# First 256 tokens of the first two projection chunks taken unnormed, their norm factor multiplied into the results

## The chip, the cores and the metric

One core of a Trainium2 chip runs the program. The metric is the device time of one execution in microseconds, as the median of several runs. Lower is better. TensorE (PE) multiplies matrices, VectorE (DVE), ScalarE (ACT) and GpSimd (POOL) work element by element, SyncE (SP) issues most of the DMAs. Each engine works through its own queue in the order in which the instructions stand there; semaphores hold an instruction back until what it needs is done.

## The reference

A residual block of a streaming encoder over 512 tokens of 1024 features, in float32. Cut to what matters here:

```python
xn = rmsnorm(h, norm_mix_g)                   # per token: x * rsqrt(mean(x*x) + eps) * g
u  = xn @ w_in                                # 1024 x 7168
q, k, v, xr, gr, ga, gb = split(u)            # seven parts of 1024 columns
ya = chunked_band_attention(q, k, v) @ w_attn_out
xc = causal_depthwise_conv(xr, conv_w, conv_b)        # four taps over the tokens
yb = (rg_lru(xc, ...) * gelu(gr)) @ w_rnn_out
h  = h + (sigmoid(ga + ..) * ya + sigmoid(gb + ..) * yb) @ w_o
h  = h + swiglu(rmsnorm(h));  out = rmsnorm(h)
```

`rmsnorm` multiplies each token's row by one number, its norm factor, and each feature by g. The factor of a token commutes with the product with `w_in`; the factor g of a feature doesn't.

## The kernel before

**Tiles.** Tokens lie in four tiles of 128 rows, `xt[0]` to `xt[3]` (names `x` in the profile), features in eight slices of 128 (k = 0 to 7). The projection needs x with the features on the partitions: `xnT[k]` holds slice k of all 512 tokens. Every operand is kept as two parts, a high part rounded to a shorter format (`fp32r`) and a low part, the rest; a product is three matrix products, high by high, high by low, low by high (`mm3`, L78 to L84). High parts are made by ACT, low parts by DVE, as a subtraction.

**Chunks.** `w_in` is taken in chunks of 256 columns, in the order xr0, gr0, ga0, gb0, xr2 and so on. A chunk's weights come by two DMAs of 512 KB (`raw`, three buffers), are split into `whl` (four buffers), and make two result tiles of 128 columns in PSUM, c = 0 and 1. Result tiles named `po_...` take turns in the four banks of the tag "mm".

**The start (L472 to L798).** Tokens are handled in two halves of 256. The first half: ACT sums the squares of tile 0 (`first_sum`, L620), DVE and ACT those of half of tile 1 each (`second_sum`, L628; `root_of_second`, L634); roots and reciprocals give the factors `rs`; DVE and ACT scale the rows into `xs` (`scaled_rows`, L651; `second_rows`, L645). TensorE turns 128x128 blocks of `xs` by a product with the identity into banks of the tags "t" and "s" (`turned`, `transposed`, L662 to L674; `pt_mix` in the profile), and `parted` (L676) multiplies by g and splits into the high and low part of `xnT`. Until this is under way, sixteen products of zeros (`busy`, L479) keep TensorE at work. Then come the products of the first half of xr0, two slices at a time (`first_pair`, L726), and of gr0 (`first_half`, L705). The second half of the tokens follows the same way, with the second half of xr0 and gr0 after it.

**After the start.** L951 to L966: xr0 goes through the convolution (`conv_in` on ACT, three `conv_taps` on DVE, `conv_out` on ACT and POOL, which gives `xch`), gr0 through the gelu (`gelu_in`, `gelu_out`, L846 to L855), meanwhile the weights of ga0 and gb0 are split (`prefetch`, L423). TensorE goes on with ga0 (`po_ga`), the gate products of the recurrence (`rg`, L867, from `xch` and the weights `wrg`) and gb0 (`po_gb`).

**What sets the order.** In the stretches under `tc.manual_schedule` the named engines keep the order of the code there, and single instructions are tied by `tc.keep_in_program_order`; the rest is placed by a scheduler. A DMA on SP waits in SP's queue for its buffer, and holds all that stand behind it.

## Time and profile before

| | us |
|---|---|
| median of 3 runs (lowest, highest) | 842.54 (841.65, 842.77) |
| the profiled execution | 842.18 |
| its span | 840.4 |
| PE busy | 833.1 |
| DVE busy | 663.2 |
| ACT busy | 516.6 |
| POOL busy | 162.5 |

The span reaches from the first to the last instruction; the time of the execution has 1.78 us more around it. A row of the timeline gives the start in us from the start of the span, the duration, the engine, the line, the operation, the tiles that it writes and reads, and their shapes; equal instructions that follow each other are one row with their count. PEld is the loading of the stationary operand, which overlaps the products. SPq is SP's DMA queue: the row is the issue, not the transfer. A matrix product's duration includes its latency, so the distance between two starts says what each costs.

### The profile page before, as it was taken

The page shows a single profiled execution, that of the slowest core. Times are in us where ns is not written, and L with a number is a line of the kernel's source. Part 1 is how long each engine was busy: PE and PEld are TensorE (multiplying, and loading weights), DVE is VectorE, ACT ScalarE, POOL GpSimd, SP SyncE. Part 2 cuts the span into 40 slices and gives each one's busy share as a digit, 9 for nine tenths or more (in the row PEclk, how much of TensorE's full clock was granted, in tenths as well). Part 3 has the DMA queues.
Part 4 walks back from the last instruction along what each step waited for, and adds up shares of the span by engine and source line. Part 5 has one row for each costly group of instructions (what it writes and reads, how often), then busy time and mean ns, then how long its engine had stood idle before and what let it go on. Part 6 is the DMA issues. An engine that isn't in the chain of part 4 may idle for free.

```text
span 840.4 us, 11922 instructions
## 1 busy us (share of the span) xinstructions
PE 833.1 (99%) x4230; PEld 706.7 (84%) x4230; DVE 663.2 (79%) x976; ACT 516.6 (61%) x850; POOL 162.5 (19%) x219
## 2 busy tenths in 40 slices
PE   9999999999999999999999999999999999999997
PEld 7988888888888888888888888888888999988886
DVE  6678769887959788887568867888778878998784
ACT  7686848774356688878534557663764465455543
POOL 2502030231010043443212012005102321300000
PEclk9999999999999999999999999999999999999999
DMA  9566488653645444548458975555955576644442
GB/s 286 172 236 224 140 301 267 184 201 100 206 145 150 138 151 139 173 129 223 97 136 220 331 283 162 165 176 165 238 175 151 147 188 183 215 155 145 160 172 100
DMA packets 107323, 153.98 MB, mean 183 GB/s; under 512 B 8216, under 2 KB 66160, under 8 KB 106752
## 3 DMA queue, kind: packets, MB, share of 16 engines
q1 hardware_dynamic: 102304, 141.32, 51.7%
q0 software_dynamic: 3728, 8.96, 6.4%
q10 hardware_dynamic: 1232, 2.95, 0.9%
q8 instruction: 33, 0.54, 0.3%
q14 instruction: 26, 0.21, 0.1%
HBM read 139.53 MB, written 30.45 MB: 202 GB/s over the span
## 4 chain that ended last, share of the span: by engine, by line
PE 98%; DMA 0%; ACT 0%; DVE 0%; issue 0%; ACTq 0%
PE fu_x L84 2%; PE fu_x L83 2%; PE fu_x L80 2%; PE o L1201 2%; PE fg_x L84 2%; PE fg_x L83 2%; PE fg_x L80 2%; PE pT L1181 2%; PE s L1152 2%; PE po_gb L80 2%; PE po_ga L80 2%; PE po_gr L84 2%; PE po_gr L80 2%; PE po_gr L83 2%; PE po_k L80 2%; PE po_q L80 2%
## 5 line engine op out<-in xcount | busy, mean ns | idle before, releaser
L1165 ACT ACTIVATE p<-p,m 128x384 f32<-128x384 f32 (+2 forms) x64 | 35.8, 560 | 14.8 <-DVE m L1164 14.3
L1170 POOL TENSOR_SCALAR p<-p,rl 128x128 f32<-128x128 f32 (+3 forms) x61 | 38.0, 640 | 15.3 <-DVE rl L1166 13.8
L1422 POOL TENSOR_TENSOR sg<-sg,keep_fu_x 128x512 f32<-128x512 f32 x8 | 14.5, 1822 | 100.3 <-DVE keep_fu_x L1421 100.3
L89 DVE TENSOR_TENSOR pp<-pT,pp 128x384 fp32r<-128x384 f32 (+1 forms) x48 | 27.0, 598 | 4.5 <-ACT pp L88 3.3
L89 DVE TENSOR_TENSOR whl_fu_w<-raw_fu_w,whl_fu_w 128x1024 fp32r<-128x1024 f32 (+1 forms) x18 | 23.4, 1307 | 8.7 <-ACT whl_fu_w L88 8.7
L89 DVE TENSOR_TENSOR whl_fu_t<-t_fu,whl_fu_t 128x1024 fp32r<-128x1024 f32 (+1 forms) x18 | 24.8, 1390 | 5.1 <-ACT whl_fu_t L88 5.0
L812 POOL MEMSET bias<- 64x64 f32 x16 | 2.4, 147 | 135.9 <-DMA bias<-ext_d 135.8
L83 PE MATMUL po_gr<-xnT,whl_gr 128*128 128x512 f32 (+1 forms) x80 | 27.6, 347 | 0.0
L80 PE MATMUL po_gr<-xnT,whl_gr 128*128 128x512 f32 (+1 forms) x80 | 27.4, 348 | 0.0
L84 PE MATMUL po_gr<-xnT,whl_gr 128*128 128x512 f32 (+1 forms) x80 | 27.2, 346 | 0.0
L1164 DVE CUSTOM_DVE_ANT_0 p<-s,bias 128x384 f32<-128x384 f32 (+2 forms) x48 | 25.4, 552 | 1.5
L88 ACT ACTIVATE whl_fu_w<-raw_fu_w 128x1024 fp32r<-128x1024 f32 (+1 forms) x18 | 17.7, 987 | 13.5 <-issue 7.6
L80 PE MATMUL po_k<-xnT,whl_qk 128*128 128x512 f32 x64 | 25.5, 398 | 0.0
L80 PE MATMUL po_q<-xnT,whl_qk 128*128 128x512 f32 x64 | 25.5, 398 | 0.0
L80 PE MATMUL po_ga<-xnT,whl_ga 128*128 128x512 f32 x64 | 25.4, 397 | 0.0
L80 PE MATMUL po_gb<-xnT,whl_gb 128*128 128x512 f32 x64 | 25.2, 394 | 0.0
L84 PE MATMUL po_q<-xnT,whl_qk 128*128 128x512 f32 x64 | 25.0, 390 | 0.0
L83 PE MATMUL po_ga<-xnT,whl_ga 128*128 128x512 f32 x64 | 25.0, 390 | 0.0
L84 PE MATMUL po_k<-xnT,whl_qk 128*128 128x512 f32 x64 | 25.0, 390 | 0.0
L80 PE MATMUL po_yb<-rnn,whl_yb 128*128 128x512 f32 x64 | 24.9, 390 | 0.0
L83 PE MATMUL po_gb<-xnT,whl_gb 128*128 128x512 f32 x64 | 24.9, 390 | 0.0
L84 PE MATMUL po_ga<-xnT,whl_ga 128*128 128x512 f32 x64 | 24.9, 389 | 0.0
(693 smaller groups left out, 3072.2 us busy)
## 6 DMA issues: line engine op xcount, KB each, us to landing
raw_qk<-in_w_in_dram SPq DMA_DIRECT2D x32, 256.0 KB, 3.3
out_t<-in_w_ffn_out_dram SPq DMA_DIRECT2D x16, 512.0 KB, 5.2
raw_fu_w<-in_w_ffn_in_dram SPq DMA_DIRECT2D x16, 512.0 KB, 4.5
raw_fo<-in_w_ffn_out_dram SPq DMA_DIRECT2D x14, 512.0 KB, 4.2
...
```

Of the source, the lines that this page charges most:

```text
L80: ins = pe.matmul(o, sh, mh, start=start, stop=False, skip_group_check=parts)
L83: pe.matmul(o, sh, ml, start=False, stop=False, skip_group_check=parts)
L84: pe.matmul(o, sl, mh, start=False, stop=stop, skip_group_check=parts)
L88: act.activation(hi, src, AF.Copy)
L89: dve.tensor_sub(lo, src, f(hi))
L1152: pe.matmul(sc, qs, kk[:, part, e, 0:w], start=part == 0, stop=part == 1, skip_group_check=qb < 2)
L1164: dve.tensor_tensor_reduce(prob[qb][:], src, prob[0][:] if qb == 0 else bias[:, S - w:S], -1.0, 3e38, ALU.add, ALU.min, nmax[:, qb:qb + 1])
L1165: act.activation(prob[qb][:], prob[qb][:], AF.Exp, bias=nmax[:, qb:qb + 1], scale=-1.0, accum_out=lsum[:, qb:qb + 1])
L1170: eng.tensor_scalar(prob[qb][:], prob[qb][:], rl[:, qb:qb + 1], 1.0, ALU.mult, ALU.mult)
L1181: pe.transpose(pt[:, at * P:(at + 1) * P], prob[qb][:, kb * P:(kb + 1) * P], ident[:])
L1201: pe.matmul(po[:, S - n:S], st, pp[i][:, part, lo:lo + n], start=kb == 0 and part == 0, stop=kb == NT - 1 and part == 1)
L1422: (pool if keep and (unit != f_units[-1] or side) else dve).tensor_mul(o, o, keep_ if keep else bank)
```

## The change

The first half of the tokens is no longer scaled before it is turned. TensorE turns the rows of x themselves, first all blocks of tile 0, then of tile 1 (`turned_by_rows`); `parted` multiplies by g as before, so that `xnT` holds x times g for the first 256 tokens, without their norm factors. With that the first halves of xr0 and gr0 are computed. The factors, still from the sums of squares, are written to DRAM as a row of 256 numbers and read back onto all partitions (`by_token`, tile `rs_b`), and DVE multiplies them into the first 256 columns of the four result tiles in PSUM before the convolution and the gelu (`scaled_first_half`). For the later chunks the first half of `xnT` is put together again (`whole_of`: high plus low), multiplied by the factors (`scaled_whole`) and split anew in place (`split_whole`), four slices at a time.

Besides: eight `busy` products in place of sixteen; the first 512 KB of weights in two DMAs; the high part of its first two slices by DVE, not ACT; in the first `first_pair` the two products of high by high first; the loads of gr0 ahead of the last two tiles of x, and those of `wrg` (`gates_loaded`) behind the factors; the split of `wrg` later; the sums of the second tile of the half later; a few instructions after the start tied to the order of the code.

```diff
...
-    def load(name, k):
+    def load(name, k, pieces=1, tied=False):
...
         for src, col, width in parts:
-            sp.dma_start(out=raw[:, :, to:to + width],
-                         in_=src[at:at + n * P, col:col + width].rearrange("(k p) e -> p k e", p=P))
+            for a in range(0, n, n // pieces):
+                b = a + n // pieces
+                ins = sp.dma_start(out=raw[:, a:b, to:to + width],
+                                   in_=src[at + a * P:at + b * P, col:col + width].rearrange("(k p) e -> p k e", p=P))
+                if tied:
+                    tc.keep_in_program_order(ins)
...
     busy = ps.tile([P, S], F32, tag="mm", bufs=4, name="busy")
-    for _ in range(16):
-        pe.matmul(busy[:], idle[:, 0:P], idle[:], start=True, stop=True)
+    for _ in range(8):
+        tc.keep_in_program_order(pe.matmul(busy[:], idle[:, 0:P], idle[:], start=True, stop=True))
...
     act.activation(warm[:], eps_t[:], AF.Sqrt)
-    load("xr0", 0)
+    load("xr0", 0, 2)
     load("xr0", 4)
+    load("gr0", 0)
...
         sp.dma_start(out=xt[t][:], in_=x[t * P:(t + 1) * P, :])
-    load("gr0", 0)
...
     wrg_raw = nm.tile([P, 8, 2, 64], F32, name="wrg_raw")
-    for n, w in enumerate((w_rg_r, w_rg_i)):
-        pairs = w.rearrange("(t two) d e -> two d t e", two=2)
-        sp.dma_start(out=wrg_raw[0:64, :, n, :], in_=pairs[0])
-        sp.dma_start(out=wrg_raw[64:128, :, 1 - n, :], in_=pairs[1])
...
-    gm_p = ps.tile([P, S], F32, tag="s", bufs=2, name="gm_p")
-    pe.transpose(gm_p[:, 0:8], gm_r[:], ident[0:8, 0:8])
...
+    def turned_by_rows(half, xs, jps, between):
+        sets = [banks_of(half, jp) for jp in jps]
+        for i in range(2):
+            for jp, pts in zip(jps, sets):
+                for j in range(2):
+                    tc.keep_in_program_order(
+                        pe.transpose(pts[j][:, i * P:(i + 1) * P], xs[i][:, (jp + j) * P:(jp + j + 1) * P], ident[:]))
+            if i == 0:
+                between()
+        return sets
...
-        def part(k, n, eng):
+        def part(k, n, eng, high=None):
...
             hi, lo, src = tiles[k // 4][:, 0, at], tiles[k // 4][:, 1, at], raws[name, k - k % 4][:, at]
-            act.activation(hi, src, AF.Copy)
+            if high:
+                high.tensor_copy(hi, src)
+            else:
+                act.activation(hi, src, AF.Copy)
...
+    spread_kk = [None]
+    rs_d = dr.tile([2, P], F32, name="rs_d")
+    def by_token(rs):
+        tc.keep_in_program_order(sp.dma_start(out=rs_d[:].rearrange("i p -> p i"), in_=rs[:]))
+        b = spread_kk[0] = qkp.tile([P, 8, 256], F32, tag="kk", bufs=1, name="rs_b")
+        src = rs_d[0:1, 0:P]
+        tc.keep_in_program_order(sp.dma_start(
+            out=b[:, 4], in_=bass.AP(tensor=src.tensor, offset=src.offset, ap=[[0, P], [1, 256]])))
+        return b[:, 4:5]
+    def gates_loaded():
+        for n, w in enumerate((w_rg_r, w_rg_i)):
+            pairs = w.rearrange("(t two) d e -> two d t e", two=2)
+            tc.keep_in_program_order(sp.dma_start(out=wrg_raw[0:64, :, n, :], in_=pairs[0]))
+            tc.keep_in_program_order(sp.dma_start(out=wrg_raw[64:128, :, 1 - n, :], in_=pairs[1]))
+    wholes = {}
+    def halves_of(k, part):
+        return xn_all[:, k:k + 4, part, 0:256]
+    def whole_of(k):
+        wholes[k] = spread_kk[0][:, 0:4] if k else qkp.tile([P, 4, 256], F32, tag="qk", bufs=1, name="whole0")[:]
+        dve.tensor_add(wholes[k], f(halves_of(k, 0)), f(halves_of(k, 1)))
+    def scaled_whole(k, rs_b):
+        dve.tensor_mul(wholes[k], wholes[k], rs_b.to_broadcast([P, 4, 256]))
+    def split_whole(k):
+        act.activation(halves_of(k, 0), wholes[k], AF.Copy)
+        dve.tensor_sub(halves_of(k, 1), wholes[k], f(halves_of(k, 0)))
+    def scaled_first_half(po):
+        dve.tensor_mul(po[:, 0:256], po[:, 0:256], rs_b[:, 0])
...
                 first[name, c] = mm_tile(f"po_{name}_{c}")
-        for xp, kinds in ((0, (0, 1)), (1, (0,))):
-            for k in (k0, k0 + 1):
-                for wpart in kinds:
-                    for c in range(2):
-                        ins = pe.matmul(first[name, c][:, 0:256], made[index[name]](wpart, k, slice(c * P, (c + 1) * P)),
-                                        xnT[k][:, xp, 0:256], start=k + xp + wpart == 0, stop=k + xp == KT)
-                        tc.keep_in_program_order(ins)
+        order = [(0, 0, k0), (0, 1, k0), (0, 0, k0 + 1), (0, 1, k0 + 1), (1, 0, k0), (1, 0, k0 + 1)]
+        if k0 == 0:
+            order[1:3] = order[2:0:-1]
+        for xp, wpart, k in order:
+            for c in range(2):
+                ins = pe.matmul(first[name, c][:, 0:256], made[index[name]](wpart, k, slice(c * P, (c + 1) * P)),
+                                xnT[k][:, xp, 0:256], start=k + xp + wpart == 0, stop=k + xp == KT)
+                tc.keep_in_program_order(ins)
...
     with tc.manual_schedule(engines={mybir.EngineType.Activation, mybir.EngineType.DVE, mybir.EngineType.Pool}):
-        xs = scaled_tiles(0)
-        q, sd, rs = row_sums(0)
-        first_sum(0, q, sd, rs)
+        q, sd, rs0 = row_sums(0)
+        gm_p = ps.tile([P, S], F32, tag="mm", bufs=4, name="gm_p")
+        pts = turned_by_rows(0, xt, (0, 2), lambda: tc.keep_in_program_order(
+            pe.transpose(gm_p[:, 0:8], gm_r[:], ident[0:8, 0:8])))
+        first_sum(0, q, sd, rs0)
         second_sum(0, q)
-        root_of_second(0, q, sd)
-        scaled_rows(0, 0, xs, rs, low)
-        second_rows(0, xs, rs, sd)
         xr0 = chunk_in_parts("xr0")
-        xr0(0, 2, dve)
+        xr0(0, 2, dve, dve)
         act.copy(gm[:], gm_p[:, 0:8])
-        pts = [*turned(0, xs, 0), *turned(0, xs, 2)]
...
         first_pair("xr0", 0)
-        scaled_rows(0, 0, xs, rs, high)
-        scaled_rows(0, 1, xs, rs, high, act)
         xr0(2, 2, dve)
+        load("gr0", 4, tied=True)
         parted(0, 2, pts[1])
-        pts = turned(0, xs, 4)
+        pts = turned(0, xt, 4)
         first_pair("xr0", 2)
-        pts += turned(0, xs, 6)
+        pts += turned(0, xt, 6)
...
         gr0 = chunk_in_parts("gr0")
+        root_of_second(0, q, sd)
+        dve.reciprocal(rs0[:, 1:2], sd[:, 1:2])
...
         parted(0, 6, pts[1])
+        rs_b = by_token(rs0)
+        gates_loaded()
...
         q, sd, rs = row_sums(1)
+        first_sum(1, q, sd, rs)
         second_sum(1, q)
+        scaled_rows(1, 0, xs, rs, low)
         gr0(4, 4, dve)
-        first_sum(1, q, sd, rs)
-        scaled_rows(1, 0, xs, rs, low)
         root_of_second(1, q, sd)
-        act.activation(wrg[:, 0], wrg_raw[:].rearrange("p t a e -> p t (a e)"), AF.Copy)
...
         second_rows(1, xs, rs, sd)
+        scaled_rows(1, 1, xs, rs, high, act)
         first_half("gr0", range(4, 7))
+        whole_of(0)
         vectors()
-        pool.tensor_sub(wrg[:, 1], wrg_raw[:].rearrange("p t a e -> p t (a e)"), f(wrg[:, 0]))
...
         parted(1, 2, pts[1])
-        scaled_rows(1, 1, xs, rs, high, act)
+        scaled_whole(0, rs_b)
+        whole_of(4)
...
         parted(1, 6, pts[1])
+        split_whole(0)
+        act.activation(wrg[:, 0], wrg_raw[:].rearrange("p t a e -> p t (a e)"), AF.Copy)
+        pool.tensor_sub(wrg[:, 1], wrg_raw[:].rearrange("p t a e -> p t (a e)"), f(wrg[:, 0]))
+        scaled_whole(4, rs_b)
+        split_whole(4)
...
-        dve.scalar_tensor_tensor(u, tr[:], 1.0, u, ALU.add, ALU.mult)
+        ins = dve.scalar_tensor_tensor(u, tr[:], 1.0, u, ALU.add, ALU.mult)
+        if j < 2:
+            tc.keep_in_program_order(ins)
...
         dve.scalar_tensor_tensor(u, u, 2.0, u, ALU.subtract, ALU.mult)
-        dve.scalar_tensor_tensor(ti[:], ti[:], 1.0, xc[:], ALU.add, ALU.mult)
+        ins = dve.scalar_tensor_tensor(ti[:], ti[:], 1.0, xc[:], ALU.add, ALU.mult)
+        if j < 2:
+            tc.keep_in_program_order(ins)
...
         po = tile_of(f"g{'ab'[w]}{j - j % 2}", j % 2, "t" if j < 2 and w == 0 else "mm")
-        act.activation((ta, zB)[w][j], po[:], AF.Tanh, bias=hb[:, 16 + 8 * w + j:17 + 8 * w + j], scale=0.5)
+        ins = act.activation((ta, zB)[w][j], po[:], AF.Tanh, bias=hb[:, 16 + 8 * w + j:17 + 8 * w + j], scale=0.5)
+        if j < 2 and w == 0:
+            tc.keep_in_program_order(ins)
...
         prefetch(index["ga0"] + 1)
+        scaled_first_half(po[0])
...
         conv_taps(0, po[0], xc[0])
+        scaled_first_half(po[1])
...
         po = [tile_of("gr0", c, ahead=0) for c in range(2)]
+        scaled_first_half(po[0])
...
         xch.append(conv_out(1, xc[1]))
+        scaled_first_half(po[1])
...
```

TensorE at the start: before, from the last warm-up product on. `xs_mix` are the scaled rows of the two tiles, `pt_mix` the turned blocks, `gm_p` the vector g turned.

```order
L480 MATMUL busy<-idle 128x512
L559 MATMUL gm_p<-ident,gm_r 128x8
L667 MATMUL pt_mix_0t<-ident,xs_mix_185 128x128
L667 MATMUL pt_mix_0t<-ident,xs_mix_186 128x128
L667 MATMUL pt_mix_0s<-ident,xs_mix_185 128x128
L667 MATMUL pt_mix_0s<-ident,xs_mix_186 128x128
L667 MATMUL pt_mix_2t<-ident,xs_mix_185 128x128
L667 MATMUL pt_mix_2t<-ident,xs_mix_186 128x128
L667 MATMUL pt_mix_2s<-ident,xs_mix_185 128x128
L667 MATMUL pt_mix_2s<-ident,xs_mix_186 128x128
L735 MATMUL po_xr_0_224<-xnT,whl_xr_0_203 128x256
```

The same place now. `x_116` and `x_117` are the two tiles of x as loaded.

```order
L484 MATMUL busy<-idle 128x512
L674 MATMUL pt_mix_0t<-ident,x_116 128x128
L674 MATMUL pt_mix_0s<-ident,x_116 128x128
L674 MATMUL pt_mix_2t<-ident,x_116 128x128
L674 MATMUL pt_mix_2s<-ident,x_116 128x128
L797 MATMUL gm_p<-ident,gm_r 128x8
L674 MATMUL pt_mix_0t<-ident,x_117 128x128
L674 MATMUL pt_mix_0s<-ident,x_117 128x128
L674 MATMUL pt_mix_2t<-ident,x_117 128x128
L674 MATMUL pt_mix_2s<-ident,x_117 128x128
L786 MATMUL po_xr_0_205<-xnT,whl_xr_0_196 128x256
```

The turning reads x itself, and tile 0 is done with before tile 1 is asked for; it stands behind eight warm-up products rather than sixteen.

DVE after the start: before, from the convolution's taps to the second gelu's end. `xc` is the convolution's sum, `g` the gelu's, the two numbers of each are c = 0 and 1.

```order
L833 SCALAR_TENSOR_TENSOR xc_547<-po_xr_0_224,vc,xc_547 128x511
L833 SCALAR_TENSOR_TENSOR xc_547<-po_xr_0_224,vc,xc_547 128x510
L833 SCALAR_TENSOR_TENSOR xc_547<-po_xr_0_224,vc,xc_547 128x509
L833 SCALAR_TENSOR_TENSOR xc_552<-po_xr_1_225,vc,xc_552 128x511
L833 SCALAR_TENSOR_TENSOR xc_552<-po_xr_1_225,vc,xc_552 128x510
L833 SCALAR_TENSOR_TENSOR xc_552<-po_xr_1_225,vc,xc_552 128x509
L850 SCALAR_TENSOR_TENSOR g_608<-g_608,po_gr_0_310 128x512
L850 SCALAR_TENSOR_TENSOR g_614<-g_614,po_gr_1_311 128x512
L89 TENSOR_TENSOR whl_gb_0_617<-raw_gb_0_618,whl_gb_0_617 128x1024
L89 TENSOR_TENSOR whl_gb_4_622<-raw_gb_4_623,whl_gb_4_622 128x1024
L855 SCALAR_TENSOR_TENSOR g_608<-g_608,po_gr_0_310 128x512
L855 SCALAR_TENSOR_TENSOR g_614<-g_614,po_gr_1_311 128x512
```

The same place now, from the first multiplication in PSUM. `rs_b` holds the factors, and beside them the second four slices of x put together.

```order
L764 TENSOR_TENSOR po_xr_0_205<-po_xr_0_205,rs_b 128x256
L761 TENSOR_TENSOR xnT<-rs_b,xnT 128x4x256
L891 SCALAR_TENSOR_TENSOR xc_547<-po_xr_0_205,vc,xc_547 128x511
L891 SCALAR_TENSOR_TENSOR xc_547<-po_xr_0_205,vc,xc_547 128x510
L891 SCALAR_TENSOR_TENSOR xc_547<-po_xr_0_205,vc,xc_547 128x509
L764 TENSOR_TENSOR po_xr_1_206<-po_xr_1_206,rs_b 128x256
L891 SCALAR_TENSOR_TENSOR xc_553<-po_xr_1_206,vc,xc_553 128x511
L891 SCALAR_TENSOR_TENSOR xc_553<-po_xr_1_206,vc,xc_553 128x510
L891 SCALAR_TENSOR_TENSOR xc_553<-po_xr_1_206,vc,xc_553 128x509
L764 TENSOR_TENSOR po_gr_0_302<-po_gr_0_302,rs_b 128x256
L908 SCALAR_TENSOR_TENSOR g_610<-g_610,po_gr_0_302 128x512
L764 TENSOR_TENSOR po_gr_1_303<-po_gr_1_303,rs_b 128x256
```

A multiplication stands ahead of each first reader of a result tile, and the second split of `xnT` between the first of them and the taps. The gelu's last products, which end the use of the banks of `po_gr`, follow further behind.

SP's queue after the first loads: before.

```order
L492 DMA x_118<-in_x_dram 128x1024
L492 DMA x_119<-in_x_dram 128x1024
L172 DMA raw_gr_0_158<-in_w_in_dram 128x4x256
L498 DMA wrg_raw<-in_w_rg_r_dram 64x8x64
L499 DMA wrg_raw<-in_w_rg_r_dram 64x8x64
L498 DMA wrg_raw<-in_w_rg_i_dram 64x8x64
L499 DMA wrg_raw<-in_w_rg_i_dram 64x8x64
L172 DMA raw_gr_4_343<-in_w_in_dram 128x4x256
L172 DMA raw_ga_0_538<-in_w_in_dram 128x4x256
```

And now. `rs_d` is the row of factors in DRAM.

```order
L174 DMA raw_gr_0_149<-in_w_in_dram 128x4x256
L497 DMA x_118<-in_x_dram 128x1024
L497 DMA x_119<-in_x_dram 128x1024
L174 DMA raw_gr_4_221<-in_w_in_dram 128x4x256
L734 DMA rs_d<-rs_mix_175 128x2x1
L174 DMA raw_ga_0_537<-in_w_in_dram 128x4x256
L174 DMA raw_ga_4_542<-in_w_in_dram 128x4x256
L737 DMA rs_b<-rs_d 128x256
L744 DMA wrg_raw<-in_w_rg_r_dram 64x8x64
L745 DMA wrg_raw<-in_w_rg_r_dram 64x8x64
```

The gr0 loads come forward, `wrg` goes behind, and the factors' way back stands behind the second load of ga0.

## The prediction

> **What bounds the kernel now.** I read the page first (busy shares and the chain that ended last), then the stretches by stage, then the timeline of each engine over the first 60 us. Two lines of the page and two stretches (bounds, length, busy us of PE, weight loads, DVE, ACT and POOL, granted clock, DMA):
>
> ```profile
> PE 833.1 (99%) x4230; PEld 706.7 (84%) x4230; DVE 663.2 (79%) x976; ACT 516.6 (61%) x850; POOL 162.5 (19%) x219
> PE 98%; DMA 0%; ACT 0%; DVE 0%; issue 0%; ACTq 0%
> 0.00:8.90 8.90, 7.59 (x25) 3.16 (x25) 2.87 (x11) 5.16 (x12) 4.95 (x14) 1.00 0.83 284
> 60.00:840.40 780.40, 774.45 (x3874) 657.30 (x3872) 621.47 (x907) 471.81 (x775) 142.35 (x173) 1.00 0.59 180
> ```
>
> TensorE (PE) is the chain almost throughout. After 60 us it misses 6 us of 780, in the tail, which the change leaves alone. So time can be won only before PE gets going, and lost wherever PE now waits. Of the 7.59 us of PE before 8.90, most is warm-up, as the timeline shows (start, duration, engine, line, operation, tiles, count; in brackets the idle time before it and who ended it):
>
> ```profile
> 1.18 6.22 PE L480 MATMUL busy<-idle 128*128 128x512 bf16 x16 [1.18 <-DVE eps_t L486]
> 7.95 0.14 PEld L667 LDWEIGHTS pt_mix_0t<-ident,xs_mix 128*128 128x128 f32 x1 [0.32 <-DVE xs_mix L656]
> 8.90 1.71 PE L735 MATMUL po_xr<-xnT,whl_xr 128*128 128x256 f32 x12
> 10.34 0.25 PEld L667 LDWEIGHTS pt_mix_4t<-ident,xs_mix 128*128 128x128 f32 x2
> 10.77 1.60 PEld L735 LDWEIGHTS po_xr<-xnT,whl_xr 128*128 128x128 f32 x12
> 15.50 0.28 PE L80 MATMUL po_gr<-xnT,whl_gr 128*128 128x256 f32 x1
> 15.62 0.28 PE L83 MATMUL po_gr<-xnT,whl_gr 128*128 128x256 f32 x1
> ```
>
> Real products start at 8.90, and from there a 256-wide one starts every 0.12 us (15.50 to 15.62). Nothing can be won beyond the distance from 8.90 to the earliest possible start, plus some 0.2 us of waits before 15.50.
>
> **The start.** The first row is from the list of SP's waits, the others from the timeline; they say what the first product can wait for once the norm is out of its way.
>
> ```profile
> SPq L499 <- DMA x<-in_x_dram: 0.8, 1, 0.8
> 6.17 0.62 SPq L499 DMA_DIRECT2D wrg_raw<-in_w_rg_r_dram  x1
> 4.65 1.06 ACT L624 ACTIVATE junk_a<-x 128x1024 f32<-128x1024 f32 x1 [1.81 <-DMA x<-in_x_dram]
> 6.24 0.67 DVE L632 CUSTOM_DVE_ANT_0 junk_c<-x 128x512 f32<-128x512 f32 x1
> 7.58 0.63 ACT L695 ACTIVATE whl_xr<-raw_xr 128x512 fp32r<-128x512 f32 x1 [0.27 <-DMA raw_xr<-in_w_in_dram]
> 8.25 0.69 DVE L696 TENSOR_TENSOR whl_xr<-raw_xr,whl_xr 128x512 fp32r<-128x512 f32 x1
> 8.38 0.47 ACT L679 ACTIVATE xnT<-pt_mix_0t,gm 128x256 fp32r<-128x256 f32 x1
> 8.88 0.48 DVE L681 SCALAR_TENSOR_TENSOR xnT<-pt_mix_0t,gm,xnT 128x256 fp32r<-128x256 f32 x1
> 9.29 0.47 DVE L681 SCALAR_TENSOR_TENSOR xnT<-pt_mix_0s,gm,xnT 128x256 fp32r<-128x256 f32 x1
> 19.09 0.88 DVE L656 TENSOR_SCALAR xs_mix<-x,rs_mix 128x512 f32<-128x512 f32 x2
> ```
>
> The first x tile landed at 4.65 and the second, by SP's wait for it, at 6.17. The loads ahead of them don't change. Eight warm-up products at the 0.4 us of the old sixteen end at 4.6, so the first tile is turned as it lands, at no cost. The second is turned from 6.17. From ready rows to ACT took 0.43 us (7.95 to 8.38), so ACT starts at 6.6 and the high part of x stands at 7.07.
>
> Weights: the whole 512 KB stood at 7.58. I put its first half midway to the x tile before it, at 6.9. DVE is free then (6.24 and some 0.6 us). The cast on DVE has no row: between 0.44 (half of 0.88) and 0.69. It is one input and one output like the first, so I take 0.44, which gives 7.35 and a first product at 7.4, 1.5 us sooner. PE then waits for DVE inside the first twelve: the low weights need 0.63 more (8.25 to 8.88), so 8.0; the low x parts end at 8.45 and 8.85, so the last two products end their slots at 9.07. Before, that point was 10.34: 1.27 us gained, 0.2 of the 1.5 lost.
>
> Then 36 products at 0.12 and eight transposes at 0.43 for four (10.34 to 10.77), 5.2 us, reach the end of the first chunk's half at 14.25. Before it was 15.50 and two deferred products, 15.74, so the lead is 1.49. ACT and DVE need 1.3 us a pair of slices against PE's 1.9, and keep ahead. The order now puts the second half of the row sums into ACT just ahead of the last weights, and the two deferred products no longer cover the next wait:
>
> ```profile
> 7.02 0.29 ACT L639 ACTIVATE sd_mix<-ssq 128x1 f32<-128x1 f32 x1
> 11.79 1.00 SPq L172 DMA_DIRECT2D raw_gr<-in_w_in_dram  x1
> 13.57 1.06 ACT L695 ACTIVATE whl_gr<-raw_gr 128x1024 fp32r<-128x1024 f32 x1
> 14.67 1.23 DVE L696 TENSOR_TENSOR whl_gr<-raw_gr,whl_gr 128x1024 fp32r<-128x1024 f32 x1
> 16.43 1.06 ACT L695 ACTIVATE whl_gr<-raw_gr 128x1024 fp32r<-128x1024 f32 x1 [1.79 <-DMA raw_gr<-in_w_in_dram]
> ```
>
> ACT: sums and root 10.4 to 11.45 (what 6.18 to 7.3 took), last weights and two x parts to 12.7, gr weights to 13.75; DVE's low part at 15.0. PE has used its four products without it by 14.73 and waits 0.3. **Lead after it: 1.2 us.** The other half of gr, awaited until 16.43 before, is now issued once a buffer is free (9.4) and takes the 4.6 us it took (11.79 to 16.43): 14.0, asked for at 15.0, hidden.
>
> **The middle.** The factor goes to DRAM and back. Its return is queued on SP behind a load that waits for DVE's 15.0; with 4.6 us it stands at 19.7. It is wanted by 23.0: DVE's next x parts (26.97 below) then come at 25.8, less two operations of 1.14 and 0.5 of small ones. Behind it on SP stand the wrg loads, wanted from 28 on, and those of gb, wanted at 42. The two sums of the halves and the first product with the factor lie in DVE's idle time at the ends of these rows:
>
> ```profile
> 25.11 0.17 DVE L583 TENSOR_SCALAR sp_e<-sp_e 128x8 f32<-128x8 f32 x1 [1.67 <-ACT sp_e L581]
> 26.97 0.48 DVE L681 SCALAR_TENSOR_TENSOR xnT<-pt_mix_4t,gm,xnT 128x256 fp32r<-128x256 f32 x1 [1.46 <-ACT xnT L679]
> 27.91 1.07 ACT L88 ACTIVATE whl_ga<-raw_ga 128x1024 fp32r<-128x1024 f32 x1
> 31.55 1.62 ACT L826 ACTIVATE xc<-po_xr,vc 128x512 f32<-128x512 f32 x2 [1.22 <-PE po_xr L84]
> 32.36 4.54 DVE L833 SCALAR_TENSOR_TENSOR xc<-po_xr,vc,xc 128x511 f32<-128x511 f32 x6 [0.78 <-ACT xc L826]
> 34.83 0.40 PE L80 MATMUL po_ga<-xnT,whl_ga 128*128 128x512 f32 x1
> 35.06 0.40 PE L83 MATMUL po_ga<-xnT,whl_ga 128*128 128x512 f32 x1
> 35.31 0.58 ACT L849 ACTIVATE g<-po_gr 128x512 f32<-128x512 f32 x1
> 39.42 2.36 DVE L89 TENSOR_TENSOR whl_gb<-raw_gb,whl_gb 128x1024 fp32r<-128x1024 f32 x2 [0.26 <-ACT whl_gb L88]
> 41.70 1.28 DVE L855 SCALAR_TENSOR_TENSOR g<-g,po_gr 128x512 f32<-128x512 f32 x2
> 47.42 0.50 PE L80 MATMUL po_gb<-xnT,whl_gb 128*128 128x512 f32 x1
> ```
>
> From here on DVE is hardly idle. ACT's high part of the scaled x begins at 26.7 (27.91 less the lead) and stands at 27.8. DVE then runs split, product, ga, ga at 1.14 each (two gb in 2.36, less the pipe's end): 32.4. A multiply in place and the second split: 33.9. Three taps at 0.76: 36.2. Multiply 0.4, ACT's 0.8, three taps: 39.8. Multiply and ACT's 0.6: 40.9. The g product 0.6, multiply, ACT: 42.6. ACT's high part of gb, 1.0: 43.6. Two gb subtractions: 45.9. The gelu product: 46.6. The multiply of 256 columns in PSUM has no row; its ends are 0.40 (8.88 to 9.29) and 0.69, and I take the first, also 256 wide from PSUM. po_ga doesn't suffer: PE comes at 33.6, the first slices are split at 29.0, and the later ones (34.0) are wanted at 36.8. The gate products need ACT's cast of 41.6 and POOL's low part of it, and PE comes at 44.6. But po_gb takes the bank of po_gr, which the first gelu product frees: at 42.3 before, with PE coming at 47.42; now at 46.6, with PE coming at 46.2. **PE waits some 0.4 us.** ACT's two added operations and wrg moved behind them are inside these times; the weights of the chunk after gb come later by as much, and PE asks for those at 57.
>
> **Sum.** 1.5 − 0.2 + 0.2 − 0.3 − 0.4 = 0.8 us won. The profiled execution took 842.18 (span 840.4 and 1.78 around it), 0.36 below the median 842.54: 841.4 for it, 841.7 for the median. That is 0.1%; under 0.2% (1.7 us) a measurement of this kernel cannot tell it from no change.
>
> **The rivals.**
> *All waits vanish.* A cheap cast, cheap multiplies and no wait at the bank leave 1.5 and the 0.2 us: 840.8, the most the start allows, just past 0.2%. For it: the bank's margin is small. Against: three separate waits must go. 0.13.
>
> *TensorE stays at half speed.* The clock is told by spacing, since the granted clock reads 1.00 there:
>
> ```profile
> 6.27 0.15 PEld L480 LDWEIGHTS <-idle 128*128 128x128 bf16 x1 [0.28 <-issue]
> ```
>
> At 6.27 a 512-wide warm-up product still took 0.43 us (0.15 and 0.28), against 0.23 later (34.83 to 35.06). So some 5.2 us of unbroken work came before full speed. Now unbroken work ends at 4.6, and transposes and gaps follow until 7.4. If 5.2 us must be served again, 24 products at 0.22 are done by 12.6 that full speed would do in 2.9. That is 2.3 lost, of which 0.5 covers waits counted above: 843.5. For it: half the warm-up is gone. Against: the gap is 2.8 us and has transposes in it. 0.15. The Trainium skill, "TensorE: Matmul & The Clock Gate", Part 1, says that full speed needs a busy window of about 3.4 us at a phase of its own, and Part 4 that transposes don't count as busy. By that rule this rival comes in those executions whose windows fall badly, at its 843.5; the trace agrees that the start is slow, with 5.2 us, and no row here shows whether transposes count.
>
> *DVE falls further behind.* In one place a subtraction of the same size, 1.23 elsewhere, ran long:
>
> ```profile
> 58.63 1.00 POOL L891 TENSOR_SCALAR a<-u 128x512 f32<-128x512 f32 x1 [1.75 <-DVE u L889]
> 59.08 1.63 DVE L340 TENSOR_TENSOR o_b<-o_b,o_b 128x1024 fp32r<-128x1024 f32 x1
> ```
>
> If the seven large operations between 27.9 and 46 cost 1.63 (POOL beside them) and the four multiplies 0.69, the bank comes 2.9 + 1.1 = 4.0 later and PE waits for all of it: 845.7. It is slower than before from 0.8 us on and measurably from 2.5. Against: two subtractions of this size kept to 2.36 (39.42). 0.12.
>
> *The split load lands no sooner.* If the first half stands only at 7.58, the start gains 0.8 and not 1.5: 842.4. 0.10.
>
> **How the numbers follow.** The forecast has the other 0.50. Faster: 0.13. Slower: 0.12. Within 0.2%: 0.75, the half-speed case included. The range leaves out most of the DVE rival and the edge of the fast one: 840.7 to 844.2.
>
> **What would show it.** Right: eight warm-up products to 4.6, the second tile's transposes at 6.2, first product at 7.4, first po_gr at 14.3, po_gb near 46.6 with DVE as its releaser. Wrong: 0.22 spacing of the first products, a factor that DVE waits for near 22, or a PE wait before po_ga.

## The result and the profile after

| | before, us | after, us |
|---|---|---|
| median (lowest, highest) of 6 runs | 842.18 (841.65, 842.77) | 852.24 (850.56, 855.08) |
| the profiled execution | 842.18 | 852.21 |
| its span | 840.4 | 850.4 |

The kernel is slower: ratio 1.0123, with a 95% interval of 1.0104 to 1.0141. The prediction of 841.7 (840.7 to 844.2) was wrong: the time lies above its range, and it went up where a small gain was forecast.

The page of the kernel after, busy time by engine and the chain that ended last. PE is busy 1.4 us longer than before, though it has eight instructions less, and its span is 10.0 us longer: it waits, and for a part of the time it runs slower. Its share of the chain fell from 98% to 89%; DVE, ACT and a DMA came in.

```profile
PE 834.5 (98%) x4222; PEld 707.8 (83%) x4222; DVE 669.8 (79%) x983; ACT 516.8 (61%) x850; POOL 165.2 (19%) x219
...
PE 89%; DVE 4%; ACT 3%; DMA 2%; issue 1%; SPq 0%; ACTq 0%; DVEq 0%
```

The waits of PE, in total, times and longest. Two are new and large, each of them one single wait.

```profile
PE rg L925 <- ACT xch L895: 3.8, 1, 3.8
PE po_xr L80 <- ACT xnT L689: 3.6, 1, 3.6
```

The stretches show where they lie (bounds, length, busy us of PE, weight loads, DVE, ACT and POOL, granted clock, DMA share, GB/s). After 100 us PE misses 5.7 us in its tail, about as before; the granted clock is below 1 in the two stretches that hold the waits.

```profile
...
15.50:31.60 16.10, 12.49 (x96) 12.29 (x95) 9.48 (x20) 6.38 (x16) 2.79 (x8) 0.89 0.56 139
31.60:60.00 28.40, 28.26 (x160) 24.07 (x159) 19.44 (x26) 21.23 (x31) 13.41 (x23) 1.00 0.52 168
60.00:100.00 40.00, 36.19 (x155) 28.36 (x154) 34.38 (x39) 28.98 (x39) 9.82 (x7) 0.96 0.66 223
100.00:850.40 750.40, 744.68 (x3739) 633.31 (x3737) 597.63 (x879) 448.79 (x744) 134.21 (x168) 1.00 0.58 178
```

Where the 10.0 us come from is read by following one PE instruction of both kernels at a time. At the second half's first turned block the kernel after is 1.1 us ahead (19.74 against 20.85): that is the start, and it came out as forecast. At the block pt_mix_4t it is 4.0 us behind (30.09 against 26.05), and still 4.0 at the first gate products `rg` (49.87 against 45.83). At the `rg` of the fifth feature tile it is 10.3 behind (135.93 against 125.61), and 10.0 at the end. So some 5.2 us go at 21 to 28 us and 6.3 at 85 to 96 us, and nothing worth naming elsewhere.

**The first loss.** The timeline of the start, of the factor's way and of the engines that wait on it:

```profile
7.23 1.93 PE L786 MATMUL po_xr<-xnT,whl_xr 128*128 128x256 f32 x12 [0.52 <-DVE whl_xr L706]
11.72 0.38 SPq L734 DMA_DIRECT2D rs_d<-rs_mix  x1
12.77 2.57 SPq L174 DMA_DIRECT2D raw_ga<-in_w_in_dram  x2
14.16 0.28 PE L80 MATMUL po_gr<-xnT,whl_gr 128*128 128x256 f32 x1
21.18 0.34 SPq L737 DMA_DIRECT2D rs_b<-rs_d  x1
24.20 0.32 ACTq L863 DMA_DIRECT2D ext_d<-ext  x1
24.57 0.47 ACT L689 ACTIVATE xnT<-pt_mix_0t,gm 128x256 fp32r<-128x256 f32 x1 [5.72 <-DMA raw_ga<-in_w_in_dram]
25.10 0.58 PE L80 MATMUL po_xr<-xnT,whl_xr 128*128 128x256 f32 x1 [3.60 <-ACT xnT L689]
27.84 1.23 DVE L757 TENSOR_TENSOR whole<-whole,rs_b 128x1024 f32<-128x1024 f32 x1 [1.10 <-DMA rs_b<-rs_d]
```

And the DMAs of 8 to 34 us (KB each, us from issue to landing; for two, the median). The first row is the kernel before, the others the kernel after.

```profile
raw_ga<-in_w_in_dram SPq DMA_DIRECT2D x2, 512.0 KB, 4.5
...
raw_ga<-in_w_in_dram SPq DMA_DIRECT2D x2, 512.0 KB, 11.8
...
rs_b<-rs_d SPq DMA_DIRECT2D x1, 128.0 KB, 6.6
...
rs_d<-rs_mix SPq DMA_DIRECT2D x1, 1.0 KB, 9.4
```

The write of the factors, 1 KB, takes 9.4 us; its return can be issued only when it has landed (21.18), and takes another 6.6. The loads of ga0, issued right behind the write, take 11.8 instead of 4.5. In two-us steps the DMA engines moved 19, 38 and 38 GB/s from 14 to 20 us:

```profile
14.00:16.00 2.00, 1.80 (x15) 1.59 (x14) 1.86 (x5) 1.97 (x5) 0.00 (x0) 1.00 0.09 19
16.00:18.00 2.00, 2.00 (x19) 2.00 (x19) 2.00 (x4) 0.91 (x4) 1.32 (x2) 1.00 0.20 38
18.00:20.00 2.00, 2.00 (x20) 2.00 (x19) 1.90 (x6) 0.72 (x1) 0.28 (x1) 1.00 0.22 38
22.00:24.00 2.00, 0.00 (x0) 0.00 (x0) 0.00 (x0) 0.00 (x0) 0.00 (x0) 1.00 0.88 281
```

The write's packets themselves are quick: in this trace they begin between 13.2 and 14.2 us and last 9 ns each, and yet the write counts as landed only at 21.16. In between the DMA engines move little. The first row has the packets of 13.0 to 14.6 us, those of the write among the 288 small ones; the second those of 14.6 to 16.5:

```profile
DMA packets 457, 0.17 MB, mean 109 GB/s; under 512 B 288, under 2 KB 457, under 8 KB 457
DMA packets 10, 0.01 MB, mean 5 GB/s; under 512 B 0, under 2 KB 10, under 8 KB 10
```

From 22 to 24 us every engine stands still (the last row of the table by steps). What holds them is a DMA that has nothing to do with the factor: ACT issues the write of a bias table (`ext_d`, L863) ahead of its parts of the second half. In the trace that issue waits for two semaphores, POOL's and the one on which the first load of ga0 tells of its landing; the table's write uses that one as well. So ACT, which needs neither, sits behind the ga0 load from 18.85 to 24.57, PE behind ACT's parts. From 25.10 products of 256 columns start 0.21 us apart instead of 0.12, until 28.04: half speed for 2.9 us, some 1.5 us lost. With the wait's 3.6 that is the 5.2, within 0.1.

**The second loss.** The timeline of 49 to 90 us:

```profile
49.81 0.37 SPq L174 DMA_DIRECT2D raw_xr<-in_w_in_dram  x1
52.50 5.63 ACT L937 ACTIVATE gt<-rg,hb 64x512 f32<-64x512 f32 x8
...
58.16 1.06 ACT L88 ACTIVATE whl_xr<-raw_xr 128x1024 fp32r<-128x1024 f32 x1
59.25 1.23 DVE L89 TENSOR_TENSOR whl_xr<-raw_xr,whl_xr 128x1024 fp32r<-128x1024 f32 x1 [6.00 <-ACT whl_xr L88]
60.39 1.22 DVE L333 TENSOR_TENSOR o_b<-o_b,o_b 128x1024 f32<-128x1024 f32 x1
...
88.64 0.61 ACT L895 ACTIVATE xch<-xc 128x512 fp32r<-128x512 f32 x1
89.30 1.05 PE L925 MATMUL rg<-xch,wrg 64*128 64x512 f32 x4 [3.81 <-ACT xch L895]
```

The same place before:

```profile
40.68 0.37 SPq L172 DMA_DIRECT2D raw_xr<-in_w_in_dram  x1
46.52 1.05 ACT L88 ACTIVATE whl_xr<-raw_xr 128x1024 fp32r<-128x1024 f32 x1
47.47 5.63 ACT L879 ACTIVATE gt<-rg,hb 64x512 f32<-64x512 f32 x8
47.60 1.23 DVE L89 TENSOR_TENSOR whl_xr<-raw_xr,whl_xr 128x1024 fp32r<-128x1024 f32 x1 [2.07 <-ACT whl_xr L88]
48.75 1.22 DVE L329 TENSOR_TENSOR o_b<-o_b,o_b 128x1024 f32<-128x1024 f32 x1
```

The second half of the xr2 weights takes the buffer that DVE's low part of gb0 frees. DVE is later there, so the load is issued at 49.81 instead of 40.68. ACT's cast of it stands not ahead of the eight gate activations, as before, but behind their 5.63 us, and DVE, in its fixed order, stands idle for 6.00 us before 59.25 with four sums (`o_b`, L333 to L336, 4.9 us) queued behind. PE is 4.0 late there; DVE's sums are 11.6 late (60.39 against 48.75). DVE does not catch up by then, and its fourth convolution tile comes late to PE at 89.30. PE waits 3.81, and then runs at half speed again until 92.9, which costs some 1.7 more. That makes 5.5 of the 6.3; the rest lies in small slips around the same products, and I have no single cause for it.

### The profile page after: what moved, and what is told of

Its sections match the earlier page's. It is cut to its first block, busy times and chain, and to the rows that moved or that the text cites. A ratio compares the mean times of both kernels' runs of the same rounds, so it can differ in the third digit from the quotient of the medians.

```text
span 850.4 us, 11913 instructions
## 1 busy us (share of the span) xinstructions
PE 834.5 (98%) x4222; PEld 707.8 (83%) x4222; DVE 669.8 (79%) x983; ACT 516.8 (61%) x850; POOL 165.2 (19%) x219
## 4 chain that ended last, share of the span: by engine, by line
PE 89%; DVE 4%; ACT 3%; DMA 2%; issue 1%; SPq 0%; ACTq 0%; DVEq 0%
PE fu_x L84 2%; PE fu_x L83 2%; PE fu_x L80 2%; PE o L1269 2%; PE fg_x L84 2%; PE fg_x L83 2%; PE fg_x L80 2%; PE pT L1249 2%; PE s L1220 2%; PE po_k L80 2%; PE po_q L80 2%; PE po_ya L80 2%; PE po_q L84 2%; PE po_k L84 2%; PE po_yb L84 2%; PE po_ya L83 2%
## 5 line engine op out<-in xcount | busy, mean ns | idle before, releaser
L1233 ACT ACTIVATE p<-p,m 128x384 f32<-128x384 f32 (+2 forms) x64 | 35.8, 560 | 14.7 <-DVE m L1232 14.2
L1238 POOL TENSOR_SCALAR p<-p,rl 128x128 f32<-128x128 f32 (+3 forms) x61 | 36.7, 617 | 15.6 <-DVE rl L1234 14.2
L80 PE MATMUL po_gr<-xnT,whl_gr 128*128 128x512 f32 (+1 forms) x80 | 27.7, 352 | 0.0
L84 PE MATMUL po_gr<-xnT,whl_gr 128*128 128x512 f32 (+1 forms) x80 | 27.5, 350 | 0.2 <-DVE whl_gr L709 0.2
L80 PE MATMUL po_xr<-xnT,whl_xr 128*128 128x512 f32 (+1 forms) x64 | 23.7, 373 | 3.6 <-ACT xnT L689 3.6
L80 PE MATMUL po_gb<-xnT,whl_gb 128*128 128x512 f32 x64 | 25.2, 394 | 0.1
```

Source lines behind the costliest of these rows:

```text
L80: ins = pe.matmul(o, sh, mh, start=start, stop=False, skip_group_check=parts)
L84: pe.matmul(o, sl, mh, start=False, stop=stop, skip_group_check=parts)
L1233: act.activation(prob[qb][:], prob[qb][:], AF.Exp, bias=nmax[:, qb:qb + 1], scale=-1.0, accum_out=lsum[:, qb:qb + 1])
L1238: eng.tensor_scalar(prob[qb][:], prob[qb][:], rl[:, qb:qb + 1], 1.0, ALU.mult, ALU.mult)
```

## The experiments

Two theories stood against each other at first. **A**: the factor's way through DRAM makes the whole loss, with what queues behind it. **B**: the DVE work that the change adds before 60 us makes a loss of its own, also with the factor on time. Each comparison is with the kernel before, run on the same chip; its median there was 842.16 to 842.38.

**e1: no factor.** Both transfers are gone and the factor is 1.0, so the norm factor of the first 256 tokens is left out.

```diff
-        tc.keep_in_program_order(sp.dma_start(out=rs_d[:].rearrange("i p -> p i"), in_=rs[:]))
...
-        tc.keep_in_program_order(sp.dma_start(out=b[:, 4], in_=...))
+        pool.memset(b[:, 4], 1.0)
```

> The factor's two transfers are gone: its place in SBUF is filled with 1.0, so the norm factor of the first 256 tokens is left out; every other instruction stays. Theory A (the round trip of the factor through DRAM costs the whole loss: its write holds up the loads behind it on the queue, one of which ACT waits for, and its return holds DVE): the PE wait of 3.6 us near 21 goes with the half-speed stretch behind it, DVE's first product with the factor starts before 22 instead of at 27.8, the PE wait of 3.8 us near 85 goes as well, and the time is 841.0 (840.5 to 842). Theory B (DVE is too full with the added sums and products whatever the factor does): the first wait goes, 3.6 and some 1.4 of half speed, but the second stays: 847.

847.59 (847.03 to 849.59), ratio 1.0065 (1.0051 to 1.0078). The first wait is gone and ga0's loads take 4.3. The second stays whole:

```profile
PE rg L922 <- ACT xch L892: 3.8, 1, 3.8
```

DVE again stands idle 5.99 us before the same low part (53.82). A alone falls: 4.7 of the 10 us go with the transfers, more than 5 stay. B's sum was near, but not its mechanism: DVE isn't short of time there, it stands idle behind ACT, whose cast comes after the gate activations. That the later load made the scheduler choose this order is likely, but no run tests it.

**e2: the factor turned by TensorE.** No DRAM: POOL spreads each factor along a row, two transposes and a copy by ACT bring it onto all partitions.

```diff
...
+            pool.tensor_copy(b[:, 5, i * P:(i + 1) * P], rs[:, i:i + 1].to_broadcast([P, P]))
...
+                pe.transpose(rs_p[:, i * P:(i + 1) * P], spread_kk[0][:, 5, i * P:(i + 1) * P], ident[:]))
+        act.copy(spread_kk[0][:, 4], rs_p[:])
...
```

> The factor is spread by TensorE instead of through DRAM: POOL copies the two columns of factors over 128 columns each, two transposes beside that of the small vectors turn them, ACT copies the result to its place. Nothing is left out. Theory A: 841.2 (840.5 to 842.5), both PE waits gone, 0.2 to 0.3 more than without the factor for the two transposes. Theory B: 847 as without the factor.

846.0 (845.69 to 847.18), ratio 1.0045 (1.0033 to 1.0058). The first wait is gone, and so is any wait for po_gr's bank: the gelu products come at 46.03 and 47.77, where the prediction has the first at 46.6. What is left is the second loss, as two waits for the gate products:

```profile
54.44 1.23 DVE L89 TENSOR_TENSOR whl_xr<-raw_xr,whl_xr 128x1024 fp32r<-128x1024 f32 x1 [6.00 <-ACT whl_xr L88]
81.50 1.30 PE L928 MATMUL rg<-xch,wrg 64*128 64x512 f32 x6 [1.05 <-POOL xch L899]
83.83 0.80 PE L928 MATMUL rg<-xch,wrg 64*128 64x512 f32 x2 [1.03 <-POOL xch L899]
```

The factor's way is thus worth 6.2 us of the kernel after (852.24 to 846.0). By e1 it is 4.7; there the second loss is larger, one wait of 3.8 with some 5 us at half speed behind it (84 to 89 us) where e2 has 2.1 with some 3.

**e3: the table's write on another queue,** so that ACT doesn't stand behind it.

```diff
-    act.dma_start(out=ext_d[:], in_=ext[:])
+    pool.dma_start(out=ext_d[:], in_=ext[:])
```

> Only the write of the bias table goes from ACT's queue to POOL's, so ACT no longer waits for the load of ga0 to land. Theory A: the wait before 25.1 goes, but DVE still stands at 27.8 for the factor ahead of the parts that TensorE wants at 26, so a wait of some 4 to 5 us appears there instead, the one near 85 stays, and the time is 852 (850.5 to 853). Rival (ACT's wait alone is the first loss, DVE's wait for the factor costs TensorE nothing): 5 us less, 847.

852.4 (849.66 to 854.62), ratio 1.0117 (1.0095 to 1.0139): nothing won. ACT is free, but DVE now stands at its product with the factor, with the low parts that PE needs behind it:

```profile
30.63 1.23 DVE L757 TENSOR_TENSOR whole<-whole,rs_b 128x1024 f32<-128x1024 f32 x1 [6.92 <-DMA rs_b<-rs_d]
```

and among PE's waits:

```profile
PE po_xr L83 <- DVE xnT L691: 3.7, 1, 3.7
```

**e4: e3, and the product with the factor behind the last parts of the second half,** so that neither ACT nor DVE stands in PE's way.

```diff
-        scaled_whole(0, rs_b)
-        whole_of(4)
...
         parted(1, 6, pts[1])
+        scaled_whole(0, rs_b)
+        whole_of(4)
```

> The table's write goes to POOL's queue and, besides, DVE's first product with the factor and the sum behind it go after the parts of the last four slices; the round trip keeps its length. Theory A in its strict form (only who stands in the queue behind the trip matters, not its length): the factor at 27.8 comes just when DVE turns to it, both PE waits go or the second shrinks under 2 us, and the time is 841.5 to 844. If the length of the trip costs by itself, as the delay of DVE's chain: the second wait stays at 2 us or more and the time is 845 or more.

850.13 (849.48 to 851.23), ratio 1.0093 (1.008 to 1.0107). The wait moves on once more, to the bank that the prediction spoke of:

```profile
PE po_gb L80 <- DVE g L913: 4.9, 1, 4.9
PE rg L925 <- ACT xch L895: 0.9, 1, 0.9
```

The factor is there at 27.5 and the gelu product at 52.28, 6.3 later than in e2. Part of that is a second split of 3.42 us (more below) and three gate activations that the scheduler put ahead of the gelu. In these two runs the queue in which the factor is waited for decides mainly where PE loses the time; the sum fell by 2.1 us at most.

**e5: e2 with the o_b sums first.** Their code goes ahead of the gate activations', so that the four sums stand ahead of the low part that DVE waited for.

```diff
             if j == w == 0:
+                sums_kept(obp, "o", 0)
                 gates_of(j)
-        sums_kept(obp, "ooff"[j // 2], j // 2 % 2)
+        if j:
+            sums_kept(obp, "ooff"[j // 2], j // 2 % 2)
```

> As the version with the factor turned on TensorE; besides, the four sums of the output weights on DVE (and their loads) are written ahead of the second half of the xr2 weights instead of behind it, so that DVE does them in the 6.0 us in which it waited there for ACT. Nothing is left out. Theory C (the second loss is this empty stretch: DVE stands behind ACT's eight gate activations with work at hand, and is that much late at the next pair): DVE is some 4.8 us earlier from there on, the two waits of 2.1 us near 82 go and the half speed behind them, and the time is 841.4 (840.8 to 842.2). Theory B (DVE has too much to do before the next pair, wherever the work stands): the waits shrink by less than half, 845.

842.8 (841.22 to 843.93), ratio 1.0006 (0.9997 to 1.0015): the same as before. The cast is where it was, behind the gates, but DVE uses the time, and PE waits for nothing after the start:

```profile
49.50 1.22 DVE L333 TENSOR_TENSOR o_b<-o_b,o_b 128x1024 f32<-128x1024 f32 x1
55.57 1.23 DVE L89 TENSOR_TENSOR whl_xr<-raw_xr,whl_xr 128x1024 fp32r<-128x1024 f32 x1 [1.20 <-ACT whl_xr L88]
```

Filling DVE's idle 6 us removes the second loss, so they were its cause: 3.2 us here (846.0 to 842.8). In its profile the first twelve products took 2.71 us instead of 1.93, so TensorE was at half speed there.

**e6: e5 with the four multiplications in PSUM in pairs, ahead of the taps.**

```diff
         scaled_first_half(po[0])
         xc = [conv_in(0, po[0])]
-        conv_taps(0, po[0], xc[0])
         scaled_first_half(po[1])
         xc.append(conv_in(1, po[1]))
+        conv_taps(0, po[0], xc[0])
         xch = [conv_out(0, xc[0])]
+        pr = [tile_of("gr0", c, ahead=0) for c in range(2)]
+        for p in pr:
+            scaled_first_half(p)
         conv_taps(1, po[1], xc[1])
...
```

> As the run before it, and the four products of the factor with the sums in PSUM are done in pairs and ahead of the taps of the convolution, so that ACT isn't waited for between them (2.4 us of DVE's empty time near 36 to 43). Nothing is left out. Theory C: nothing is left to gain by it but some margin: the same within 0.3 us, 841.4. If the chain of DVE still holds TensorE anywhere between 45 and 90 (a bank, the gate products): up to 0.8 us less than the run before it.

841.72 (840.93 to 847.51), ratio 1.0 (0.9988 to 1.0012). Its profiled run, at 847.51, began at half speed (2.87 for the twelve) and has a wait of 2.5 at `fg_x` that ends at 686 us (the expectation of e14 puts it near 673), far from the change. I have no cause for that one.

**e7: the kernel after with e5's move of the sums (its diff alone), and nothing else.**

> The changed kernel with its round trip through DRAM, and only the sums of the output weights moved ahead of the second half of the xr2 weights. Theory A and C together (two losses, each with its own cause): the wait of 3.6 near 21 and its half speed stay, that of 3.8 near 85 goes with its half speed, some 6 us less than the changed kernel: 846.2 (845.5 to 847.5). If the second wait hangs on the first (DVE late because of the factor): it shrinks by the 4.8 us that DVE gains only where it was under that, and stays in part: 848 or more.

846.72 (844.31 to 847.86), ratio 1.0052 (1.0038 to 1.0065). Only the first wait is left:

```profile
PE po_xr L80 <- ACT xnT L689: 3.0, 1, 3.0
```

So the order is worth 5.5 us of the kernel after, the factor's way 6.2, and both together 9.4 (852.24 to 842.8); the parts sum to 11.7. That the late factor also makes DVE later would explain some of it, but the starts at half speed vary between these runs too, so the division is rough.

**e8: the factors written as 128 pairs.** The tile in DRAM is [128, 2], so that each packet has 8 B. The numbers then stand in another order, and the factors meet other tokens.

```diff
-    rs_d = dr.tile([2, P], F32, name="rs_d")
+    rs_d = dr.tile([P, 2], F32, name="rs_d")
...
-        tc.keep_in_program_order(sp.dma_start(out=rs_d[:].rearrange("i p -> p i"), in_=rs[:]))
+        tc.keep_in_program_order(sp.dma_start(out=rs_d[:], in_=rs[:]))
...
```

> The factor's write goes out as 128 pairs of 8 bytes instead of 256 single values; the return is unchanged, so the factors meet other tokens than their own. If each small packet has its price: the write lands in 5 to 6 us instead of 9.4, the load of ga0 behind it at about 20 instead of 24, the factor by 24, the first wait is under 1 us, and the time is 847. If the write's 9.4 us are the queue ahead of it, or a fixed latency: as the changed kernel, 852, with the same 9 us.

One run, 848.69.

```profile
raw_ga<-in_w_in_dram SPq DMA_DIRECT2D x2, 512.0 KB, 8.7
rs_b<-rs_d SPq DMA_DIRECT2D x1, 128.0 KB, 8.2
...
rs_d<-rs_mix SPq DMA_DIRECT2D x1, 1.0 KB, 4.9
```

Half as many packets take half the time (9.4 to 4.9) with the same bytes, and the first wait shrinks from 3.6 to 0.3: by this run the cost lies in the number of packets or their size of 4 B, which change together here, and not in the bytes or a fixed latency. The Trainium skill, "DMA: Bandwidth & Descriptors", Rules for kernel authors, says that a last dimension that isn't contiguous becomes one descriptor per element; these two times agree.

**e10: the write of the factors on ACT's queue.**

```diff
-        tc.keep_in_program_order(sp.dma_start(out=rs_d[:].rearrange("i p -> p i"), in_=rs[:]))
+        tc.keep_in_program_order(act.dma_start(out=rs_d[:].rearrange("i p -> p i"), in_=rs[:]))
```

> The changed kernel, with the factor's write to DRAM given to ACT's queue instead of SP's; the return stays on SP. Nothing is left out. If the write holds up what stands behind it on its own queue: the two loads of ga behind it land in 4.5 to 6 us instead of 11.8 while the write itself still takes 8 to 9, ACT waits less than 1 us for the load of ga0, and the first wait of PE turns into one on DVE's parts near 26 as with the table on the other queue. If the write keeps all transfers of the core waiting, whatever the queue: the loads of ga still take 11 to 12 us.

One run, 854.59. The loads of ga0 on SP's queue are held up all the same:

```profile
raw_ga<-in_w_in_dram SPq DMA_DIRECT2D x2, 512.0 KB, 12.8
...
rs_d<-rs_mix ACTq DMA_DIRECT2D x1, 1.0 KB, 9.2
```

The Trainium skill, same page, Issuing engines are not separate DMA queues, says that DMAs of all issuers run on the same 16 engines; 12.8 beside 4.5 agrees. In what way so few bytes hold the others up, no run here shows.

**e12: the kernel before with an unread write of 256 values,** on SP between the loads of gr0 and ga0.

```diff
         gr0(4, 4, dve)
+        rs_d = dr.tile([2, P], F32, name="rs_d")
+        tc.keep_in_program_order(sp.dma_start(out=rs_d[:].rearrange("i p -> p i"), in_=rs0[:]))
```

> The kernel before with nothing added but the write of the first 256 factors to DRAM, 256 single values, on SP between the loads of gr0 and ga0; nobody reads it. It measures the write alone: 8 to 9.5 us to landing, the two loads of ga 11 to 12 us instead of 4.5, landing near 24 to 26, ahead of the 27.9 at which ACT asks for the first; the table's write follows another lane there and does not wait, so the time is that of before, 842.2 (841.7 to 843.2). If the write by itself costs time in before too: 843.5 or more.

One run, 842.11: nothing lost, though the write takes 9.6 us and the load of ga0 8.9 (11 to 12 were expected). There ACT asks for ga0 only at 28.2, and the table's write is issued at 22.24, as good as before (21.94). The trip's price lies in who waits for it.

**e11: e2 without the ties to code order after the start,** in three places.

```diff
-        if j < 2:
-            tc.keep_in_program_order(ins)
```

> As the version with the factor turned on TensorE, without the five ties that the change puts on the first pair's gate and u operations. Nothing is left out. Theory C: the second half of the xr2 weights still stands behind ACT's eight gate activations, since its load waits for DVE, so DVE's 6 us stay empty and the time stays within 1 us of 846.0. If the ties set that order: 842 or less.

845.64 (844.95 to 846.23), ratio 1.0039 (1.0026 to 1.0053). The cast still stands behind the gates (54.88), so the ties don't set that order. The equal time is partly luck, though: DVE's idle time there is 4.1 us in three pieces and no wait for the gate products near 82 is left, while a new wait of 2.3 came up at po_gb, whose bank DVE frees 2.1 us later than in e2.

**e9, e13, e14: the clock at the start.** Three warm-up products more after the first tile's transposes, and three after the second's, fill the gaps in which TensorE waits for x.

```diff
...
+            filler(3)
...
         pts = turned_by_rows(0, xt, (0, 2), between)
+        filler(3)
```

e9, on e6:

> As the version with the factor turned on TensorE, the sums first and the products in pairs; besides, three warm-up products stand between the transposes of the two x tiles and three behind them, where TensorE otherwise waits some 0.7 us each. Nothing is left out. Theory D (what still varies by 2 us from one execution to the next is the clock: the two gaps before the first product lose full speed in some executions): the first twelve products take 1.9 us and not 2.7 to 2.9, the executions lie within 1 us of each other and the median is 841.1 (840.7 to 841.5). If the spread comes from elsewhere (when transfers land): the spread stays at 2 us or more and the median at 841.7 or above, as the fillers can delay the second tile by 0.2.

841.4 (841.11 to 845.71), ratio 1.0 (0.9988 to 1.0012); nine of eleven runs within 841.11 to 842.44, two at 845.1 and 845.7. In its profile the start holds full speed, and no wait is left after it:

```profile
7.29 1.92 PE L784 MATMUL po_xr<-xnT,whl_xr 128*128 128x256 f32 x12
```

e13, on the kernel after:

> The changed kernel with its round trip and its order, and only the fillers: three warm-up products between the transposes of the two x tiles and three behind them. Nothing is left out. Theory D (in some executions of the changed kernel full speed is lost in the gaps before its first product, at 1.5 to 2 us each time): the median falls by 0.3 to 1.2 us to 851.0 to 851.9, and executions above 853 (two of six before) become rare. If the spread of the changed kernel comes from when the factor's write lands (8.3 to 9.4 us seen): median and spread as before, 852.2 and 850.6 to 855.

851.94 (851.49 to 853.97), ratio 1.012 (1.0104 to 1.0135); its waits are 3.8 and 3.4. The median is 0.3 us lower, which is well within the spread of both, and one of four executions is still near 854.

e14, on e5:

> The version with the factor turned on TensorE and the sums first, with the fillers, and the products with the factor left in the order of the changed kernel. Nothing is left out. Theory D: every execution at full speed from the first product, 841.4 (841.0 to 841.9) against 842.8 without the fillers. The few executions of 845 that the version with the products in pairs had, with a wait near 673 in a stage that no edit touches: if they belong to that order they don't come here; if they come too, they belong to the shift of the later stages against the clock or the transfers, and not to the pairs. If the fillers gained nothing: 842.8.

842.06 (841.39 to 843.0), ratio 0.9996 (0.9987 to 1.0005). The spread falls from 2.7 us to 1.6, and no run is near 845. Such runs came with the multiplications in pairs only, 3 of 23 (e6, e9) against 0 of 22 (e5, e14), too few to say that they belong to them. All three filled versions have a start at full speed in their one profile; without the fillers seven of eleven profiles have.

No version is measurably faster than the kernel before. The best median, 841.4, is 0.1% below it.

## Why the prediction was wrong, step by step

**The start: right.** First product 7.23 (forecast 7.4), the first twelve in 1.93 against 1.71 before (0.2 lost, as forecast), end of the half 14.16 (14.25), the wait for gr's low part 0.20 (0.3), lead 1.11 (1.2).

**The factor's way: the step that failed.** The prediction says: "Its return is queued on SP behind a load that waits for DVE's 15.0; with 4.6 us it stands at 19.7." That prices the return alone and gives the write no time. The return waits not only for the load ahead of it (issued at 14.97) but for the write's landing. The runs put 8.3 to 9.6 us on a write of 256 single values, and 6.6 to 7.7 on its return (4.6 in the prediction). 11.72, 9.4 and 6.6 make 27.7, and DVE got the factor at 27.84. No row of the profile before had such a write, and I put no bounds on it, though for the other unknown prices I did. That it also holds up the loads behind them, and through the shared semaphore ACT's table write, is the other half: "ACT's two added operations and wrg moved behind them are inside these times" looked at durations only, not at what each issue waits for. One of the prediction's own signs of being wrong, a PE wait before po_ga, thus came: 3.60 us, ended at 25.10.

**The DVE chain to the bank: right.** The multiplication in PSUM took 0.42 (0.40). With the factor on time (e2) the first gelu product stands at 46.03 for 46.6. The bank wait appears as soon as DVE is later than that beside PE: 0.6 in e8, 2.3 in e11, 4.9 in e4. The kernel after has none, since PE itself is 4 us late there.

**The end of the look: the second step that failed.** "the weights of the chunk after gb come later by as much, and PE asks for those at 57", and "After 60 us it misses 6 us of 780, in the tail, which the change leaves alone". PE did have those weights in time. But ACT's cast of them fell behind 5.63 us of gate activations, DVE's 6.00 idle us there were not in the sum, and DVE's delay reached PE 30 us later. The prediction followed PE's next need of the weights and not the queue of DVE behind them.

**The rivals.** "TensorE stays at half speed" is real: in the profiles of e3, e5, e6 and e10 the first twelve products took 2.71 to 2.90 us. But in the other seven profiles of the same start they took 1.92 or 1.93, and the twelve lost 0.8 to 1.0 us where the rival's 843.5 has 1.8 above the forecast. What it costs at the median stays open: with the fillers the medians moved by 0.3 to 0.7 us (e6 to e9, after to e13, e5 to e14), each within the spread. Why it comes in some executions only, and whether transposes count as work, was not tried alone. "DVE falls further behind" had the right engine, but the wrong reason and place: in the kernel after the two splits of x took 1.24 and 1.21 and the multiplications 0.42, and DVE was late because it stood idle. "The split load lands no sooner" did not come: DVE began its cast at 6.66. "All waits vanish" was put at 840.8; e9, with both causes and the gaps of the start mended, reached 841.4 (lowest 841.11), 0.9 below the kernel before beside it. That is the size of the sum's 0.8, and in e9's profile a lead of 1.0 us lasts to the last products. But the interval of its ratio (0.9988 to 1.0012) holds no change as well, and e14 is only 0.3 below: a gain over many executions is not shown.
